# Delta rule loads kept in two fixed sets, half of the first state copies on ScalarE, and two score products moved ahead of values products

## The chip, the cores and the metric

The kernel runs on one core of a Trainium2 chip. The core has five engines that work side by side: TensorE (PE, matrix products into PSUM; its weight loads are shown apart as PEld), VectorE (DVE), ScalarE (ACT), GpSimd (POOL) and SyncE (SP, which here only issues DMA transfers). The metric is the device time of one execution in microseconds (us), a median of several runs. All numbers here come from the runs of the kernel before the change and from the trace of one profiled execution of it.

## What is computed

A two-layer backbone over 512 latent tokens and 256 context tokens of width 1024. Layer 0 mixes tokens with a bidirectional gated delta rule, layer 1 with grouped-query attention (8 query heads, 2 key heads, width 128); each is modulated, gated and added to the stream, and the latent stream is normed at the end. The two places that matter here, cut from the reference:

```python
# layer 0: per head and direction, chunks of 64 tokens, state s (128 x 128)
def step(s, xs):
    qk_i, qd_i, kd_i, u_i, w_i, gl_i = xs
    v_new = u_i - jnp.einsum('bhcd,bhde->bhce', w_i, s)
    o = jnp.einsum('bhcd,bhde->bhce', qd_i, s) + jnp.einsum('bhcs,bhse->bhce', qk_i, v_new)
    s = s * gl_i[..., None, None] + jnp.einsum('bhcd,bhce->bhde', kd_i, v_new)
    return s, o

# layer 1: attention of the latent tokens over context and latent tokens
s = jnp.einsum('bqhgd,bkhd->bhgqk', qg, k).astype(F32) * (d ** -0.5)
p = jax.nn.softmax(s, axis=-1).astype(v.dtype)
return jnp.einsum('bhgqk,bkhd->bqhgd', p, v).reshape(b, lq, hq, d)
```

## The kernel before

**The delta rule.** Both directions run at once: a tile of 128 rows holds one chunk of 64 tokens for the forward direction and one for the backward direction. There are six such tiles (two of context, four of latent tokens) and each is visited twice, with the two halves in exchanged roles, so there are 12 steps; `where(s)` gives the tile and the visit of step `s`. The tiles of steps 0 to 11 are 0, 1, 1, 0, 2, 3, 4, 5, 5, 4, 3, 2. Each step has four units of four value heads (`x = 4 * s + p`), 48 in all. A unit goes through three functions in three successive rounds of one loop: `products(x)` multiplies keys (`kq[0]`) and queries (`kq[1]`) with the state `St` on TensorE, forms `r` on VectorE from the values and `o` on ScalarE, and decays the state on GpSimd; `solve(x)` applies the inverted matrix `T` and copies the new values `vn` and their decayed form `vd`; `update(x)` multiplies with `QK` for the output and with `kt` for the new state, `su`. In one round TensorE gets the products of unit x, the solve of x-1 and the update of x-2, in that order. In step 0 the state is zero, so there are no products with keys and queries, and `su` is copied to the state (line 1660) instead of added.

**Its loads.** `load_step(s)`, called with the first unit of a step, loads from DRAM what the step reads: k, q, kt, `T` and `QK` of 512 KB each, and the values in two transfers of 512 KB. Even steps use one set of buffers (tiles of the pool `even`), odd steps another (tags `T`, `v`, `QK`, `kt`, `kq0` of the pool `ch`), and q has two buffers of its own (`kq1`), used in turn. Every step from 1 on loads everything, also where a set held the same tile before. Only step 0 has its tiles loaded earlier (`opening`). The loads are issued by SyncE.

**What sets the order.** The work of TensorE, VectorE, ScalarE and GpSimd around the change is in an order written out by hand (`written0`, and `written` in layer 1): each of these engines runs its instructions in the order in which the code traces them. SyncE's queue is not written out there; a scheduler orders it. `mark[0]` keeps the last load of a step; the first output weights and gates are issued after it (`tc.issue_after(mark[0])` at units 28, 32, 36 and 40).

**The scores of layer 1.** 32 units `u` (8 heads by 4 tiles of 128 queries) run through a loop. `scores(u)` computes 768 scores per query in three passes of products (the float32 operands are split into a high and a low part). Two units share three PSUM banks in the tile `s3`: each has a bank for itself (`own`, 512 columns) and half of the bank between them (`shared`, 256 columns). Then come `maxima(u)` on VectorE, `powers(u)` (the exponentials, line 2275) on ScalarE, and two units later the transposes `turn`. `values(u2, kts)` multiplies shares with values, half of a pair of units per round of the loop. Up to u = 23 each round also has a projection for TensorE, from u = 26 on a block of the output product; u = 24 and 25 have neither.

Of the kernel before, what the change touches and what calls it, by code (L numbers as in the profile page):

```python
# [8 lines left out]
F32 = mybir.dt.float32  # L9
# [8 lines left out]
P = 128  # L18
# [5 lines left out]
QH, VH = 8, 16  # L24
# [62 lines left out]
def backbone(tc, a, out):  # L87
    nc = tc.nc
    V, S, G, T = nc.vector, nc.scalar, nc.gpsimd, nc.tensor
    dma = nc.sync.dma_start  # L90
# [16 lines left out]
    k_d = dtile([NT, P, QH, P], "k_d")  # L107
    q_d = dtile([NT, P, QH, P], "q_d")
    kt_d = dtile([NT, P, QH, P], "kt_d")
# [4 lines left out]
    t_d = dtile([NT, P, 2, VH, 64], "t_d")  # L114
    qk_d = dtile([NT, P, 2, VH, 64], "qk_d")
# [887 lines left out]

    def matrices_loaded(t, visit, Tt, QK, kt):
        dma(Tt, t_d[t, :, visit])
        dma(QK, qk_d[t, :, visit])
        return dma(kt, kt_d[t]).ins

    def values_loaded(t, v, h0=0, h1=VH):
        p, n, base = pair_info(t)  # L1010
        for hf, c in ((0, p), (1, n - 1 - p)):
            c += base // 64
            dma(v[hf * 64:hf * 64 + 64, h0:h1], v_d[c // 2, c % 2 * 64:c % 2 * 64 + 64, h0:h1])

    def values_tile(s):
        return room["even"].tile([P, 2, 32, 32], F32, tag="C", name=f"cv_{s}").rearrange("p a b c -> p (a b c)").rearrange("p (h d) -> p h d", d=P)

    def even_tile(s, nm):
        return room["even"].tile([P, VH, 64], F32, tag="df", name=f"c{nm}_{s}", bufs=4)

    def by_key_heads(x):
        return x.rearrange("p h c -> p (h c)").rearrange("p (h d) -> p h d", d=P)

    opening = {}
# [117 lines left out]
    last = {}  # L1142
    T0 = 134
# [33 lines left out]
    ck = Piece("DVE", 0.4, 0.0, biases_kept, after=[pv], holds=[("tr", pv)], lands=0.1, slack=0.1)  # L1177
# [17 lines left out]
    for q in range(4):  # L1195
# [7 lines left out]
        for k in (2 * q, 2 * q + 1):  # L1203
            y_ = None
            for i in range(2):
                f = at + 2.5 * (k % 2) + 0.6 * i
# [18 lines left out]
    for k in range(KT):  # L1225
        for h in steps:
            wh, wl = halves_of[h]
            for i in range(2):
                first = not k
# [20 lines left out]
    for h in range(QH):  # L1250
# [4 lines left out]
        else:  # L1255
            wh, wl = k_weights(h, t0)
            g, owners = [], []
            for i in range(2):
                n = 1 if h == 1 else 4
# [28 lines left out]
    c = []  # L1288
# [29 lines left out]
    for n, (i, nb) in enumerate(((0, 4), (0, 5), (1, 0), (1, 2), (1, 1), (1, 3), (1, 4), (1, 5))):  # L1318
# [3 lines left out]
        first, through = nb >= 4 or nb < 2, []  # L1322
# [93 lines left out]
    for pair in range(3):  # L1416
        first = None
# [5 lines left out]
    for t in range(NT):  # L1423
        due = T0 + (185, 80, 315, 190, 30, 335)[t]
        U = [Piece("DVE", 2.15, due, j_turn, t, d, after=[solved[t // 2]] + (joined if t < 5 else []), takes=["U" if t < 5 else "U5"] if d == 0 else (), lands=0.1) for d in range(2)]
        u = U[0].takes[0]
# [96 lines left out]
    if True:  # L1523
        ch.tile([P, 4, P], F32, tag="r0", name="r_0", bufs=1)
        St = [ch.tile([P, 2, 2, P], F32, tag=f"S{hh}", name=f"S{hh}", bufs=1) for hh in range(QH)]
        for tag, shape, n in (("vn", [P, 4, P], 2), ("vd", [P, 4, P], 2), ("T", [P, VH, 64], 1), ("v", [P, VH, P], 1), ("QK", [P, VH, 64], 1),
                              ("kt", [P, QH, P], 1), ("kq0", [P, QH, P], 1), ("kq1", [P, QH, P], 2), ("o", [P, 4, P], 2), ("r1", [P, 4, P], 1)):
            for i in range(n):
                ch.tile(shape, F32, tag=tag, name=f"{tag}_first{i}", bufs=n)

        def where(s):
            n, sl, base = (4, s, 0) if s < 4 else (8, s - 4, 2)
            visit = 0 if sl < n // 2 else 1
            return base + (sl if visit == 0 else n - 1 - sl), visit

        loads = {}
        mark = [None]

        def load_step(s):
            nm = f"_{s}"  # L1540
            t, visit = where(s)
            if s == 0:
                (Tt, QK, kt), v = opening["m"], opening["v"]
                loads[s] = (None, kt, v, Tt, QK)
                return
            if s % 2:
                Tt = ch.tile([P, VH, 64], F32, tag="T", name="cT" + nm, bufs=1)
                v = ch.tile([P, VH, P], F32, tag="v", name="cv" + nm, bufs=1)
                QK = ch.tile([P, VH, 64], F32, tag="QK", name="cQK" + nm, bufs=1)
                kt = ch.tile([P, QH, P], F32, tag="kt", name="ckt" + nm, bufs=1)  # L1550
            k0 = ch.tile([P, QH, P], F32, tag="kq0", name="ck" + nm, bufs=1) if s % 2 else by_key_heads(even_tile(s, "k"))
            if not s % 2:
                Tt, QK = even_tile(s, "T"), even_tile(s, "QK")
                kt, v = by_key_heads(even_tile(s, "kt")), values_tile(s)
            kq = [k0, ch.tile([P, QH, P], F32, tag="kq1", name="cq" + nm)]
            for w, src in enumerate((k_d, q_d)):
                dma(kq[w], src[t])
            values_loaded(t, v)
            mark[0] = matrices_loaded(t, visit, Tt, QK, kt)
            loads[s] = (kq, kt, v, Tt, QK)  # L1560

        live = {}
        prq = [pcx.tile([P, 2, 4, P], F32, tag=tag, name=f"{tag}_all", bufs=1) for tag in ("pr", "pq")]
# [63 lines left out]
        def update(x):  # L1629

            s, p = divmod(x, 4)
            t, visit = where(s)
            kq, kt, v, Tt, QK = loads[s]
            vn, vd = live.pop(x)
            po = prq[x % 2][:, :, 2:4]
            for i in range(2):
                for j in range(2):
                    for hf in range(2):
                        r0, i0 = hf * 64, (hf ^ j) * 64
                        T.matmul(po[r0:r0 + 64, j, i], QK[i0:i0 + 64, 4 * p + 2 * j + i, :], vn[i0:i0 + 64, 2 * j + i], start=True, stop=True)  # L1640
            if s < 11:
                su = pux.tile([P, 2, 2, 2, P], F32, tag="su", name=f"su{x}", bufs=1)
                for j in range(2):
                    hh = 2 * p + j
                    for c0 in (0, 64):
                        for d in range(2):
                            r0 = (visit ^ d ^ j) * 64
                            T.matmul(su[c0:c0 + 64, d ^ j, j], kt[r0:r0 + 64, hh, c0:c0 + 64], vd[r0:r0 + 64, 2 * j:2 * j + 2], start=True, stop=True)  # L1648
            oh = O[t][:, 4 * p:4 * p + 4]
            ov = oh.rearrange("p (j i) d -> p j i d", j=2)  # L1650
            if s == 0:
                S.copy(ov, po)
            else:
                V.tensor_tensor(ov, po, ov, ALU.add)
            if s < 11:
                for j in range(2):
                    hh = 2 * p + j
                    sj = raw(su[:, 0, 0] if j == 0 else su[:, 1, 1], 0, [[512 - 1024 * j, 2], [P, 2], [1, P]])
                    if s == 0:
                        V.tensor_copy(St[hh], sj)  # L1660
                    else:
                        V.tensor_tensor(St[hh], sj, St[hh], ALU.add)  # L1662

# [586 lines left out]
        z_tanh(hq)  # L2250
        z_rest(hq)

    def scores(u):
        hq, t = divmod(u, 4)
        g, b = hq // 4, u % 2
        own, shared = (slice(0, 512), slice(512, 768)) if b == 0 else (slice(256, 768), slice(0, 256))
        for c in (own, shared):
            for n_, (i, j) in enumerate(PASS):
                q = qTs[hq // 2][i][:, hq % 2, t * P:(t + 1) * P]
                T.matmul(s3[:, b, c], q, kT[j][:, g, c], start=n_ == 0, stop=n_ == 2)  # L2260
# [119 lines left out]
    for u in range(32 + 4):  # L2380
# [32 lines left out]
        for half in range(2):  # L2413
            if piece and piece[0] is q_products:
                q_products(*piece[1:], range(half * 4, half * 4 + 4))
            elif piece:
                k0 = 4 * (u % 2) + 2 * half
                z_products(piece[1], range(k0, k0 + 2))
            elif half == 0 and 26 <= u < 33:
                out_block(u - 26, 0, pg)  # L2420
            elif half == 0 and u >= 33:
                s_all = raw(s3, 0, [[1, 3 * 512]])
                acc1 = [s_all[:, nh * 512:(nh + 1) * 512] for nh in range(2)]
                for k in ((0, 1, 2), (3, 4, 5), ())[u - 33]:
                    out_block(k, 1, acc1)
                if u == 35:
                    out_block(7, 0, pg)
            if half == 1 and o is not None:
                q_turned(*last[1:], o)
            if u == 32 and half == 0:  # L2430
                aq_c.__exit__(None, None, None)
                f2_c = tc.tile_pool(name="fo", bufs=2, side="right", reuse_waits="tile")
                f2 = f2_c.__enter__()
                fg = f2.tile([P, D], F32, tag="fg", name="fg", bufs=1)
                gate1 = f2.tile([P, 1, D], F32, tag="gate1", name="gate1", bufs=1)
                ss = f2.tile([P, 4, 3], F32, tag="ss", name="ss", bufs=1)
                dma(gate1, gate_d[1])
                for t in range(3):
                    load_hs(t)
                dma(fg, a["final_norm_g"].unsqueeze(0).partition_broadcast(P).squeeze(1))  # L2440
                G.tensor_scalar(fg, fg, -(2.0 ** 0.5), None, ALU.mult)
            if half == 1 and u >= 4:
                u2, h_ = divmod(u - 4, 2)
                values(u2, range(3 * h_, 3 * h_ + 3))
# [158 lines left out]
```

## Time and profile before

| | us |
|---|---|
| runs shown | 1145.9, 1141.11, 1144.64 |
| median of these | 1144.64 |
| the profiled execution's own time | 1139.69 |
| its span, first to last instruction | 1137.5 |
| the delta rule's stretch in it, about | 535 to 712 |
| the scores' units 24 and 25 in it, about | 1054 to 1062 |

The span of the profiled execution is a little shorter than its time, since the time also has what lies around the instructions. The page of the profile begins with the busy time of each engine; below it stand views of the trace. In a timeline each row is: start in us, duration or stretch in us, engine, line of the code, operation, output <- inputs, shapes (partitions x elements), how many were merged, and in brackets the idle time of the engine just before the row with what ended it. "issue" as a releaser means that the engine waited for nothing that the profile shows. SPq marks DMA transfers as SyncE issues them. The granted clock is the share of full speed at which TensorE was allowed to run (1.00 is full).

### The profile page before, as it was taken

The numbers are of one execution on the slowest core, as the hardware profiler recorded it, in microseconds if no ns is written. First come the engines' busy times: TensorE is split into PE (matmuls) and PEld (weight loads), VectorE is DVE, ScalarE is ACT, GpSimd is POOL, SyncE is SP. The second block draws the span as 40 slices with busy tenths as digits, with TensorE's granted clock in tenths as the row PEclk, the third lists the DMA queues.
The fourth block names the chain that finished last, engine by engine and source line by source line (L and its number), as shares of the span: only waits on it lengthen the run. The fifth ranks groups of instructions, "written<-read, shape, count | busy, mean of one in ns | idle before, by whom it ended". The sixth has DMA issues, their size and how long they took to land. (4 is left out here: it accounts for less than half of the span.)

```text
span 1137.5 us, 27228 instructions
## 1 busy us (share of the span) xinstructions
PE 1106.4 (97%) x10511; PEld 903.7 (79%) x10511; DVE 787.5 (69%) x1628; ACT 746.9 (66%) x1990; POOL 603.1 (53%) x525
## 2 busy tenths in 40 slices
PE   5999999999999999999999999999999999999997
PEld 2677788888888888888666666788877889989886
DVE  4785666688889988774678788445555477667647
ACT  4453554477787888756689888875776356666731
POOL 0564111329999999960675598656744353130820
PEclk9999999999999999999999999999999999999999
DMA  9489753765738887665998994676854112101323
GB/s 366 180 305 324 253 159 118 228 174 171 219 129 245 280 233 222 182 229 164 280 279 249 276 257 116 207 213 183 247 148 139 37 58 73 38 19 57 111 75 93
DMA packets 117106, 208.69 MB, mean 183 GB/s; under 512 B 12113, under 2 KB 76786, under 8 KB 111730
## 3 DMA queue, kind: packets, MB, share of 16 engines
q1 hardware_dynamic: 97202, 195.71, 55.8%
q10 hardware_dynamic: 19776, 11.25, 3.3%
q8 instruction: 83, 1.36, 0.5%
q14 instruction: 45, 0.37, 0.1%
HBM read 166.16 MB, written 40.67 MB: 182 GB/s over the span
## 5 line engine op out<-in xcount | busy, mean ns | idle before, releaser
L1768 PE MATMUL po<-woh,y 128*128 128x512 f32 x384 | 129.3, 401 | 0.0
L1706 POOL TENSOR_TENSOR wol<-wo,woh 128x1024 fp32r<-128x1024 f32 x32 | 77.3, 2416 | 54.3 <-ACT woh L1699 51.1
L810 POOL TENSOR_TENSOR X<-X,tmp 128x62 f32<-128x62 f32 (+15 forms) x93 | 99.5, 1070 | 7.3
L1594 POOL TENSOR_TENSOR S<-S,glb 128x512 f32<-128x512 f32 x80 | 81.8, 1044 | 36.4 <-PE ks L1585 36.1
L809 POOL TENSOR_TENSOR tmp<-L,X 128x62 f32<-128x62 f32 (+15 forms) x93 | 91.0, 979 | 6.7
L929 PE MATMUL g_z<-uh,wh_z 128*128 128x512 f32 (+1 forms) x256 | 88.0, 344 | 0.0
L929 PE MATMUL g_v<-uh,wh_v 128*128 128x512 f32 (+1 forms) x256 | 87.9, 344 | 0.0
L944 DVE SCALAR_TENSOR_TENSOR acc_v<-g_v,cwv,acc_v 128x510 f32<-128x510 f32 (+3 forms) x128 | 77.7, 614 | 14.7 <-ACT acc_v L936 11.3
L929 PE MATMUL g_z<-ul,wh_z 128*128 128x512 f32 (+1 forms) x256 | 86.2, 337 | 0.5 <-issue 0.5
L929 PE MATMUL g_v<-ul,wh_v 128*128 128x512 f32 (+1 forms) x256 | 86.1, 336 | 0.0
L929 PE MATMUL g_v<-uh,wl_v 128*128 128x512 f32 (+1 forms) x256 | 86.1, 336 | 0.0
L929 PE MATMUL g_z<-uh,wl_z 128*128 128x512 f32 (+1 forms) x256 | 86.1, 336 | 0.0
L1768 PEld LDWEIGHTS po<-woh,y 128*128 128x128 f32 x384 | 72.3, 188 | 15.5 <-issue 0.3
L1768 PE MATMUL po<-wol,y 128*128 128x512 f32 x192 | 75.5, 393 | 0.0
L1734 DVE SCALAR_TENSOR_TENSOR pt<-pt,og,z 128x128 f32<-128x128 f32 x96 | 34.4, 358 | 33.3 <-PE pt L1725 31.0
L555 POOL TENSOR_TENSOR kt<-kt,kss 128x768 f32<-128x768 f32 x8 | 11.6, 1472 | 85.6 <-DVE kss L183 57.0
L1585 PE MATMUL ks<-S,ck 128*64 128x256 f32 x352 | 55.5, 392 | 0.9 <-ACT o L1591 0.9
L1662 DVE TENSOR_TENSOR S<-su,S 128x512 f32<-128x512 f32 x80 | 51.5, 686 | 5.1 <-PE su L1648 3.4
L1588 DVE SCALAR_TENSOR_TENSOR r<-ks,negV,cv 128x128 f32<-128x128 f32 x176 | 52.4, 344 | 3.6 <-DMA cv<-v_d 1.9
L1585 PE MATMUL ks<-S,cq 128*64 128x256 f32 x352 | 53.7, 379 | 0.0
L929 PEld LDWEIGHTS g_z<-ul,wh_z 128*128 128x128 f32 x256 | 48.6, 190 | 5.4 <-issue 0.7
L929 PEld LDWEIGHTS g_z<-uh,wh_z 128*128 128x128 f32 x256 | 48.5, 190 | 5.2
(469 smaller groups left out, 3341.5 us busy)
## 6 DMA issues: line engine op xcount, KB each, us to landing
aw<-in_ada_late SPq DMA_DIRECT2D x16, 1024.0 KB, 7.5
wo<-in_dn_w_out SPq DMA_DIRECT2D x32, 512.0 KB, 3.9
cv<-v_d SPq DMA_DIRECT2D x22, 512.0 KB, 9.6
aw<-in_ada_first SPq DMA_DIRECT2D x8, 1024.0 KB, 11.4
w_z<-in_dn_w_in SPq DMA_DIRECT2D x16, 512.0 KB, 6.2
w_v<-in_dn_w_in SPq DMA_DIRECT2D x16, 512.0 KB, 4.8
v_d<-vt ACTq DMA_DIRECT2D x16, 384.0 KB, 4.2
cT<-t_d SPq DMA_DIRECT2D x12, 512.0 KB, 9.1
```

The lines of the kernel that those rows point to most:

```text
L555: G.tensor_tensor(kt, kt, bcast(r[:, h % 2 * NT:(h % 2 + 1) * NT], 2, P), ALU.mult)
L809: G.tensor_tensor(tv, bcast(L[:, :, j + 1:, j], 3, j + 1), bcast(X[:, :, j, 0:j + 1], 2, n), ALU.mult)
L810: G.tensor_tensor(X[:, :, j + 1:, 0:j + 1], X[:, :, j + 1:, 0:j + 1], tv, ALU.subtract)
L929: T.matmul(ps[:, :m], w[:, k], u[:, k, c0:c0 + m], start=k == 0 and n_ == 0, stop=k == KT - 1 and n_ == 2)
L944: V.scalar_tensor_tensor(acc[:, c0 + lo:c0 + hi], ps[:, lo + j - 2:hi + j - 2], cwv[:, j, ct:ct + 1], acc[:, c0 + lo:c0 + hi], ALU.mult, A ...
L1585: T.matmul(ks[r0:r0 + 64, w], kq[w][:, hh, r0:r0 + 64], St[hh][:, d], start=True, stop=True)
L1588: V.scalar_tensor_tensor(r[:, 2 * j + i], ks[:, 0, i], negV[:, visit, t, h:h + 1], v[:, h], ALU.mult, ALU.add)
L1594: G.tensor_tensor(St[hh], St[hh], bcast(g_, 3, P), ALU.mult)
L1662: V.tensor_tensor(St[hh], sj, St[hh], ALU.add)
L1706: G.tensor_tensor(wl, raws.pop(n), halves[n][0], ALU.subtract)
L1734: V.scalar_tensor_tensor(pj, pj, og, raw(z, off, [[st_, 2], [1, 64]]), ALU.mult, ALU.mult)
L1768: T.matmul(acc[nh], y[i][:, j, :], ww[k][:, nh * 512:(nh + 1) * 512], start=h == 0 and x == 0, stop=h == VH - 1 and x == 2)
```

## The change

Three edits.

The delta rule's k, q, values and kt now live in two fixed sets, A and B, named for each step by the string `"ABBABABAABAB"`. Steps 2, 8 and 9 use the set that an earlier step has loaded for the same tile, and load only `T` and `QK`; step 3 loads k and q but keeps the values and kt of step 0. `T` and `QK` still alternate between two buffers. For step 1 the transfer of q is issued behind the values, `T` and `QK`; for the other steps the order is k, q, values, `T`, `QK`, kt. `mark[0]` is now the last transfer that the step has.

In step 0 the second of the two state halves of a unit is copied by ScalarE (`S.copy`), the first still by VectorE.

At u = 24 and 25 the `own` products of the next unit's scores are traced at the start of the half round, ahead of the values products; the next round then traces only the `shared` ones.

```diff
@@ -1523,8 +1523,14 @@
-        for tag, shape, n in (("vn", [P, 4, P], 2), ("vd", [P, 4, P], 2), ("T", [P, VH, 64], 1), ("v", [P, VH, P], 1), ("QK", [P, VH, 64], 1),
-                              ("kt", [P, QH, P], 1), ("kq0", [P, QH, P], 1), ("kq1", [P, QH, P], 2), ("o", [P, 4, P], 2), ("r1", [P, 4, P], 1)):
+        work = [(("vn", [P, 4, P], 2), ("vd", [P, 4, P], 2)), (("o", [P, 4, P], 2), ("r1", [P, 4, P], 1))]
+        odd = {}
+        for tag, shape, n in work[0]:
+            for i in range(n):
+                ch.tile(shape, F32, tag=tag, name=f"{tag}_first{i}", bufs=n)
+        for nm, shape in (("T", [P, VH, 64]), ("v", [P, VH, P]), ("QK", [P, VH, 64]), ("kt", [P, QH, P]), ("k", [P, QH, P]), ("qB", [P, QH, P]), ("qA", [P, QH, P])):
+            odd[nm] = ch.tile(shape, F32, tag=nm, name="c" + nm, bufs=1)
+        for tag, shape, n in work[1]:
             for i in range(n):
                 ch.tile(shape, F32, tag=tag, name=f"{tag}_first{i}", bufs=n)
...
+        (T0, QK0, kt0), v0 = opening["m"], opening["v"]
+        homes = {"A": (by_key_heads(even_tile(0, "k")), odd["qA"], v0, kt0), "B": (odd["k"], odd["qB"], odd["v"], odd["kt"])}
+
         def load_step(s):
-            nm = f"_{s}"
             t, visit = where(s)
+            k, q, v, kt = homes["ABBABABAABAB"[s]]
+            Tt, QK = (odd["T"], odd["QK"]) if s % 2 else (T0, QK0)
+            loads[s] = ((k, q), kt, v, Tt, QK)
             if s == 0:
-                (Tt, QK, kt), v = opening["m"], opening["v"]
-                loads[s] = (None, kt, v, Tt, QK)
                 return
-            if s % 2:
-                Tt = ch.tile([P, VH, 64], F32, tag="T", name="cT" + nm, bufs=1)
...
-            for w, src in enumerate((k_d, q_d)):
-                dma(kq[w], src[t])
-            values_loaded(t, v)
-            mark[0] = matrices_loaded(t, visit, Tt, QK, kt)
-            loads[s] = (kq, kt, v, Tt, QK)
+            fresh = s not in (2, 8, 9)
+            if fresh:
+                dma(k, k_d[t])
+                if s > 1:
+                    dma(q, q_d[t])
+                if s != 3:
+                    values_loaded(t, v)
+            dma(Tt, t_d[t, :, visit])
+            last = dma(QK, qk_d[t, :, visit])
+            if s == 1:
+                dma(q, q_d[t])
+            if fresh and s != 3:
+                last = dma(kt, kt_d[t])
+            mark[0] = last.ins
@@ -1657,7 +1663,7 @@
                     if s == 0:
-                        V.tensor_copy(St[hh], sj)
+                        (S.copy if j else V.tensor_copy)(St[hh], sj)
@@ -2250,11 +2256,13 @@
+    begun = set()
+
-    def scores(u):
+    def scores(u, first=False):
...
-        for c in (own, shared):
+        for c in (own,) if first else (shared,) if u in begun else (own, shared):
@@ -2439,6 +2447,9 @@
+            if half == 0 and u in (24, 25):
+                scores(u + 1, first=True)
+                begun.add(u + 1)
             if half == 1 and u >= 4:
                 u2, h_ = divmod(u - 4, 2)
                 values(u2, range(3 * h_, 3 * h_ + 3))
```

More of the change, by code (lines that the diff above doesn't have):

```diff
@@ L1537, in backbone @@
         mark = [None]
+        (T0, QK0, kt0), v0 = opening["m"], opening["v"]
+        homes = {"A": (by_key_heads(even_tile(0, "k")), odd["qA"], v0, kt0), "B": (odd["k"], odd["qB"], odd["v"], odd["kt"])}
         def load_step(s):
-            nm = f"_{s}"
             t, visit = where(s)
+            k, q, v, kt = homes["ABBABABAABAB"[s]]
+            Tt, QK = (odd["T"], odd["QK"]) if s % 2 else (T0, QK0)
+            loads[s] = ((k, q), kt, v, Tt, QK)
             if s == 0:
-                (Tt, QK, kt), v = opening["m"], opening["v"]
-                loads[s] = (None, kt, v, Tt, QK)
                 return
-            if s % 2:
-                Tt = ch.tile([P, VH, 64], F32, tag="T", name="cT" + nm, bufs=1)
[L1548 to L1555, printed above, removed]
-            for w, src in enumerate((k_d, q_d)):
-                dma(kq[w], src[t])
-            values_loaded(t, v)
-            mark[0] = matrices_loaded(t, visit, Tt, QK, kt)
-            loads[s] = (kq, kt, v, Tt, QK)
+            fresh = s not in (2, 8, 9)
[12 more added lines that the diff above has]
+            mark[0] = last.ins
         live = {}
```

## The prediction

> **What bounds the kernel now.** First the head of the page, which says which engine fills the span, and the stretch of the delta rule (535 to 712 us) in the view of windows. The columns of a window are its length, the busy time of PE, PEld, DVE, ACT and POOL with instruction counts, the granted clock, the DMA share and GB/s.
>
> ```profile
> span 1137.5 us, 27228 instructions
> PE 1106.4 (97%) x10511; PEld 903.7 (79%) x10511; DVE 787.5 (69%) x1628; ACT 746.9 (66%) x1990; POOL 603.1 (53%) x525
> ...
> 557.00:572.00 15.00, 14.09 (x236) 8.91 (x232) 11.58 (x28) 10.67 (x34) 11.07 (x11) 1.00 1.02 284
> 588.00:603.00 15.00, 15.00 (x260) 9.78 (x256) 12.24 (x28) 14.27 (x53) 9.37 (x10) 1.00 0.87 273
> ```
>
> TensorE (PE) bounds it, and it does so inside the delta rule too: 15.00 of 15.00 us busy, while the DMA engines are nearly full (0.87) but in time. So a byte that is not loaded is worth something only where PE waited for it. I look for those places in the timeline of PE. One unit (four value heads of a step) begins with the products of keys and state:
>
> ```profile
> 612.71 0.65 PE L1585 MATMUL ks<-S,ck 128*64 128x256 f32 x4
> 616.48 0.65 PE L1585 MATMUL ks<-S,ck 128*64 128x256 f32 x4
> ...
> 557.30 0.65 PE L1585 MATMUL ks<-S,ck 128*64 128x256 f32 x4
> 560.67 1.13 DVE L1588 SCALAR_TENSOR_TENSOR r<-ks,negV,cv 128x128 f32<-128x128 f32 x4 [1.85 <-DMA cv<-v_d]
> 562.06 0.65 PE L1585 MATMUL ks<-S,ck 128*64 128x256 f32 x4 [0.91 <-ACT o L1591]
> ...
> 569.61 0.65 PE L1585 MATMUL ks<-S,ck 128*64 128x256 f32 x4
> 573.73 0.32 PE L1640 MATMUL pq_all<-vn,cQK 64*64 64x128 f32 x2 [1.16 <-issue]
> 574.96 0.65 PE L1585 MATMUL ks<-S,ck 128*64 128x256 f32 x4
> ...
> 646.68 0.65 PE L1585 MATMUL ks<-S,ck 128*64 128x256 f32 x4
> 651.02 0.65 PE L1585 MATMUL ks<-S,ck 128*64 128x256 f32 x4
> ```
>
> An undisturbed unit takes 616.48 - 612.71 = 3.77 us. Three units are longer. The one from 557.30 takes 4.76: VectorE waited for step 2's values, so 0.99 us too much. The one from 569.61 takes 5.35, 1.58 too much, with PE waiting for nothing that the profile shows, while the DMA engines were full (1.02 in the window above). The one from 646.68 takes 4.34, 0.57 too much. Every other start that I followed from 542 to 708 us keeps the 3.77.
>
> **Reuse of the loads.** With 512 KB in every load of one tensor (values: two of them), steps 2, 8 and 9 each lose k, q, kt and the values (2.5 MB) and step 3 loses kt and the values (1.5 MB): 9 MB in all. The sets are freed when the two buffers are freed now, since a set's next load comes two steps after its last use, so no later load has a shorter window. The first two output weights are tied to the last load of steps 7 and 8; for step 8 that is now QK instead of kt, so one of them leaves a little earlier, and nobody waits for it. I take the three excesses as gone: 0.99 + 1.58 + 0.57 = 3.1 us. The first is sure, as the load is gone. The other two happen beside a full DMA queue, and after the change steps 2, 3, 8 and 9 load far less; if they were something else, 2.1 us of the 3.1 stay.
>
> **The order of step 1's loads** is the part that I hold for decisive. The diff moves q from behind k to behind the values, T and QK. SyncE's timeline and the landing times (last column, us after the issue; the view asked once for each load) of before:
>
> ```profile
> 530.50 0.83 SPq L1557 DMA_DIRECT2D ck<-k_d  x1
> 531.38 0.42 SPq L1557 DMA_DIRECT2D cq<-q_d  x1
> 531.85 1.10 SPq L1013 DMA_DIRECT2D cv<-v_d  x2
> 533.04 0.53 SPq L1005 DMA_DIRECT2D cT<-t_d  x1
> 533.61 0.45 SPq L1006 DMA_DIRECT2D cQK<-qk_d  x1
> ...
> ck<-k_d SPq DMA_DIRECT2D x1, 512.0 KB, 4.1
> cq<-q_d SPq DMA_DIRECT2D x1, 512.0 KB, 6.6
> cv<-v_d SPq DMA_DIRECT2D x2, 512.0 KB, 8.4
> cT<-t_d SPq DMA_DIRECT2D x1, 512.0 KB, 12.8
> cQK<-qk_d SPq DMA_DIRECT2D x1, 512.0 KB, 14.9
> ...
> 542.20 0.65 PE L1585 MATMUL ks<-S,ck 128*64 128x256 f32 x4
> 542.68 0.60 PE L1585 MATMUL ks<-S,cq 128*64 128x256 f32 x4
> ```
>
> They land in the order of issue: k at 534.6, q at 538.0, the values about 540.3, T at 545.8, QK at 533.61 + 14.9 = 548.5. The queue sends them back to back from 530.5 on, so I expect the new order to leave in the same stretch, with as many bytes ahead of the last, and q, now the sixth, to land where QK lands now: 548.5. PE needs it at 542.68, and the products with q stand between those with k: PE stops there, and with it everything behind in its order (the rest of step 0's solves and updates too). That is 548.5 - 542.7 = 5.9 us of wait with the semaphore, which also swallows what the copy below gains. T and QK, which come earlier instead, were not waited for. Bounds: q in time (0) and a landing 2 us later (7.9).
>
> The Trainium skill speaks against this order of landings: in "DMA: Bandwidth & Descriptors", section "Queues, rings and completion order", completion is not first in, first out per issuing engine. By that rule q could be in time and this term 0; the five landings above, all in the order of issue, disagree with it here.
>
> A wait of this length has a second price, which one place of the trace shows:
>
> ```profile
> 24.34 2.08 PE L308 MATMUL rr<-dg,on 128*128 128x512 f32 x2 [3.76 <-DVE dg L303]
> ...
> 22.00:24.00 2.00, 0.00 (x0) 0.00 (x0) 2.00 (x1) 1.50 (x4) 1.74 (x1) 0.90 0.99 410
> 24.00:28.00 4.00, 3.66 (x10) 2.24 (x10) 2.36 (x5) 0.69 (x2) 0.00 (x0) 0.50 1.02 422
> 28.00:32.00 4.00, 4.00 (x22) 1.43 (x21) 3.69 (x15) 1.65 (x4) 0.00 (x0) 0.69 1.02 424
> ```
>
> After 3.76 us without work PE's granted clock is 0.50 for the whole window 24 to 28, and a mean of 0.69 means 0.50 for 2.5 of the next 4 us: about 6.1 us at half speed after the restart, worth up to 3.1 us. My wait is longer than that one, so I expect the same. Bounds 0 and 3.1; I take 2.1, nearer the upper end since this row is the only one, and less than it because the first unit after a wait also waits for VectorE and ScalarE. The rule in the Trainium skill's "TensorE: Matmul & The Clock Gate", section "Part 1: The HAM clock gate", that one busy window of about 3.4 us brings the clock back, would make this term an estimated 1.7 instead.
>
> **Second state halves on ScalarE.** In step 0 PE's second group of state products waits until VectorE has read both halves of the first:
>
> ```profile
> 539.43 1.29 DVE L1660 COPY S<-su 128x512 f32<-128x512 f32 x2
> 539.86 0.59 ACT L1613 COPY vn<-pr_all 128x512 f32<-128x512 f32 x1 [0.80 <-PE pr_all L1611]
> 540.86 1.41 PE L1648 MATMUL su<-vd,ckt 64*64 64x256 f32 x16 [0.64 <-DVE S L1660]
> ```
>
> With one half on each engine the pair is done after about 0.65 instead of 1.29, so PE's wait of 0.64 goes. ScalarE pays four copies of 0.59 (its row for the same shape); the next one on it, vn at 539.86, starts some 0.1 later, and its products come only after the group that waited. So up to -0.64, but only if PE does not wait for q right after: in my sum 0.
>
> **Scores ahead of values.** In the late units of layer 1 PE has no projection to fill with. The view of groups by form for 1050 to 1066, then the timeline and the chain of work:
>
> ```profile
> L2260 PE MATMUL s<-kT,qT 128*128 128x512 f32 x9 | 2.8, 418 | 1.4 <-ACT pr L2275 1.4
> L2260 PE MATMUL s<-kT,qT 128*128 128x256 f32 x12 | 2.1, 281 | 0.0
> ...
> 1058.31 1.31 PE L2260 MATMUL s<-kT,qT 128*128 128x512 f32 x6 [0.79 <-ACT pr L2275]
> 1061.99 1.32 PE L2260 MATMUL s<-kT,qT 128*128 128x512 f32 x6 [0.65 <-ACT pr L2275]
> ...
> 1065.37 1.09 PE po L2309 x9
> 1066.46 1.12 PE s L2260 x6
> ...
> 1106.86 11.20 PE pso L2471 x48
> ```
>
> The 512-column products are the bank that a unit has for itself (`own`), the 256-column ones the bank shared with its neighbour. The wait for ScalarE's reading of the other unit's scores stands before the 512-column form, 1.4 us, and none before the other: `own` already waits for the powers of the unit before, whatever the banks. Placed ahead of the values products it keeps that wait, and those nine products (1.09), which run inside the wait now, are queued behind it. PE then idles 0.79 + 1.09 and does the values afterwards. The unit's scores end about 1.07 later, so the maxima and powers and the next unit's wait move too, and the same happens once more: 2 x 1.07 = +2.1 us. The later end of the values also moves VectorE's gating of them, which stands ahead of the next maxima; some 0.1 of that may show, and I leave it to the range. Behind it PE runs without a gap to the last block (11.20 us of products from 1106.86), so it reaches the end. Bounds: if `own` did not wait, PE would fill 0.7 (its share of 1.12) of each wait: -1.4.
>
> **Sum.** +5.9 (q) + 2.1 (clock) + 2.1 (scores) - 3.1 (excesses) = +7.0 us. The profiled execution took 1139.69 us for its span of 1137.5, the median of the runs shown is 1144.64, 0.4% more; the terms are differences, so I add them to the median: 1151.6 us. Its own range is 1148 to 1155, from the 2.1 that may stay to a lower clock term.
>
> **Rivals.**
> - **q is in time** (not slower): q lands before about 542, because the queue puts it forward or the loads start some 6 us earlier. It decides from a landing at 542.7 on. For it: the order on SyncE's queue is not written out by hand as PE's is, so a load may be sent ahead of its place in the code. Against it: k, q, values, T and QK now go out in the order of the code. Then -0.6 - 3.1 + 2.1 = -1.6: 1143.0. Chance 0.17.
> - **`own` does not wait**, so the split does what it says: +5.9 + 2.1 - 3.1 - 1.4 = +3.5, 1148.1. The row with 1.4 against 0.0 speaks against it. Chance 0.06.
> - **The wait for q is longer** and the clock stays low over more units, with the 2.1 of excess kept: +7.9 + 3.1 + 2.1 - 1.0 = +12.1, 1156.7. Chance 0.05.
> - My forecast: 0.72.
>
> **Chances.** A measurement of this kernel can tell about 0.5% from no change, 5.7 us. Of the forecast's 0.72 I put 0.50 above +5.7 and 0.22 below; the long wait adds 0.05 above. Within 0.5%: 0.22 + 0.06 + 0.12 of the first rival = 0.40, the other 0.05 of which is faster by more. So slower 0.55, same 0.40, faster 0.05. The range 1142 to 1155.5 takes in most of the first rival and leaves out the long wait.
>
> **What would show it.** In the profile of the changed kernel: the products with cq of step 1 wait several us for the DMA cq<-q_d about 542 to 549, and the granted clock falls below 1.0 there; the wait for cv at the second step and the 1.16 us of issue are gone; two waits of PE for ACT pr at L2260's line are near 1.9 us instead of 0.79 and 0.65, ahead of po's products. I am wrong if cq lands before PE reaches it, if the clock stays at 1.0 through a wait over 5 us, or if the split products start before the powers end.

## The result and the profile after

| | before | changed |
|---|---|---|
| median of 8 runs each, us | 1143.28 (1139.08 to 1145.9) | 1148.47 (1147.42 to 1149.74) |
| profiled execution, us | 1139.69 | 1147.42 |
| its span, us | 1137.5 | 1145.5 |
| mean granted clock | 0.995 | 0.991 |

The changed kernel takes 1.0056 times as long, with a 95% interval of 1.0043 to 1.0069: about 6 us more (the two medians alone differ by 5.2). The forecast was 1151.6 us, and its range, 1142 to 1155.5, holds the median.

The head of the page of the changed kernel:

```profile
span 1145.5 us, 27187 instructions
PE 1109.7 (97%) x10511; PEld 906.3 (79%) x10511; DVE 787.6 (69%) x1624; ACT 751.0 (66%) x1994; POOL 603.3 (53%) x525
```

PE has as many instructions as before, so its work has not grown. 8.0 us of span must have come from places where PE stood still or ran slower. The view of waits for PE names the two that are new or have grown (us in total, times, longest; the second was 1.4 in all before the change):

```profile
PE ks L1591 <- DMA cqB<-q_d: 4.2, 1, 4.2
...
PE s L2268 <- ACT pr L2283: 3.4, 2, 1.9
```

The timeline of the changed kernel around step 1, with SyncE's (SPq), VectorE's and ScalarE's rows that bear on it:

```profile
531.52 0.43 SPq L1563 DMA_DIRECT2D cQK<-qk_d  x1
532.00 0.66 SPq L1565 DMA_DIRECT2D cqB<-q_d  x1
...
533.77 0.67 PE L1617 MATMUL pr_all<-cv,cT 64*64 64x128 f32 x16
...
537.82 0.69 DVE L1666 COPY S<-su 128x512 f32<-128x512 f32 x1
538.54 0.59 ACT L1666 COPY S<-su 128x512 f32<-128x512 f32 x1 [1.09 <-DVE S L1666]
539.18 1.08 PE L1654 MATMUL su<-vd,ckt 64*64 64x256 f32 x11 [0.56 <-ACT S L1666]
541.03 0.65 PE L1654 MATMUL su<-vd,ckt 64*64 64x256 f32 x5 [0.77 <-issue]
541.62 0.65 PE L1591 MATMUL ks<-S,ck 128*64 128x256 f32 x4
546.46 1.12 PE L1591 MATMUL ks<-S,cqB 128*64 128x256 f32 x4 [4.18 <-DMA cqB<-q_d]
...
551.97 0.65 PE L1591 MATMUL ks<-S,ck 128*64 128x256 f32 x4
...
710.90 0.65 PE L1591 MATMUL ks<-S,ck 128*64 128x256 f32 x4
```

Its landing times (last column, us after the issue) and its windows (length, the five engines' busy time, granted clock, DMA share, GB/s):

```profile
cQK<-qk_d SPq DMA_DIRECT2D x1, 512.0 KB, 12.7
cqB<-q_d SPq DMA_DIRECT2D x1, 512.0 KB, 14.4
```

```profile
540.00:544.00 4.00, 1.50 (x12) 0.40 (x9) 0.69 (x1) 0.69 (x2) 0.88 (x2) 1.00 1.02 420
544.00:548.00 4.00, 1.54 (x8) 0.98 (x10) 0.38 (x2) 0.00 (x0) 0.33 (x1) 0.53 0.83 237
548.00:552.00 4.00, 4.00 (x57) 2.52 (x54) 0.84 (x3) 2.32 (x6) 2.54 (x4) 0.62 0.44 150
...
550.00:551.00 1.00, 1.00 (x28) 1.00 (x24) 0.00 (x0) 0.96 (x3) 0.42 (x1) 0.50 0.03 12
551.00:552.00 1.00, 1.00 (x22) 0.47 (x16) 0.00 (x0) 0.73 (x2) 0.78 (x2) 0.98 0.49 111
...
1064.00:1068.00 4.00, 2.69 (x14) 2.39 (x12) 2.21 (x4) 1.75 (x4) 4.00 (x3) 0.69 0.64 229
```

QK lands at 531.52 + 12.7 = 544.2 and q at 532.00 + 14.4 = 546.4, in the order of issue. PE starts on q at 546.46. The unit from 541.62 to 551.97 takes 10.35 us where 3.77 is undisturbed. 4.18 of that is the wait, and the other 2.40 go with products at half clock: a group of four products with k or q takes 1.07 to 1.12 instead of 0.60 to 0.65, and the clock's column reads 0.53 and 0.62. In the windows of 1 us it is 0.50 up to 551 and nearly full behind it. The two rows of S show something that the diff doesn't: ScalarE's copy begins at 538.54, just after VectorE's has ended at 537.82 + 0.69 = 538.51. The halves are copied one behind the other, as before.

The late units of layer 1, after the change:

```profile
1059.41 0.81 PE L2296 MATMUL pt<-ident,pr 128*128 128x128 f32 x6
1062.08 0.96 PE L2268 MATMUL s<-kT,qT 128*128 128x512 f32 x3 [1.85 <-ACT pr L2283]
1062.89 1.99 PE L2317 MATMUL po<-pT,vv 128*128 128x256 f32 x9
...
1068.24 0.96 PE L2268 MATMUL s<-kT,qT 128*128 128x512 f32 x3 [1.55 <-ACT pr L2283]
...
1071.02 1.65 PE L2331 MATMUL pg<-wo,yT 128*128 128x512 f32 x6
```

And the marks in the timeline of the kernel before, to measure the same stretches:

```profile
545.97 0.65 PE L1585 MATMUL ks<-S,ck 128*64 128x256 f32 x4
...
707.80 0.65 PE L1585 MATMUL ks<-S,ck 128*64 128x256 f32 x4
...
1055.64 0.82 PE L2288 MATMUL pt<-ident,pr 128*128 128x128 f32 x6
...
1063.73 1.64 PE L2323 MATMUL pg<-wo,yT 128*128 128x512 f32 x6
```

The own scores (the 512-column form) stop PE ahead of the values products, twice, and the nine values products of 1062.89 take 1.99 us instead of 1.30: the clock fell here too (0.69 in the window from 1064), though not before the own scores behind the wait had run at full speed (0.96). With these marks the span is accounted for, PE's start of step 0 being 535.38 before and 533.77 after:

| stretch | before | after | difference |
|---|---|---|---|
| ahead of step 0's first solve | 535.38 | 533.77 | -1.61 |
| step 0's first solve to step 1's first unit | 6.82 | 7.85 | +1.03 |
| step 1's first unit | 3.77 | 10.35 | +6.58 |
| second unit's start to the last unit's start | 161.83 | 158.93 | -2.90 |
| from there to unit 24's transposes | 347.84 | 348.51 | +0.67 |
| unit 24's transposes to the first output block | 8.09 | 11.61 | +3.52 |
| the rest | 73.77 | 74.48 | +0.71 |

They add up to 8.00. The first row and the fifth belong to no part of the change; with the same work ahead of it, step 0 starts between 533.77 and 536.63 in the profiles of all kernels here.

### The profile page after: what moved, and what is told of

Same layout as the page of the kernel before. It is cut to its first block, busy times and chain, and to the rows that moved or that the text cites. A ratio compares the mean times of both kernels' runs of the same rounds, so it can differ in the third digit from the quotient of the medians.

```text
span 1145.5 us, 27187 instructions
## 1 busy us (share of the span) xinstructions
PE 1109.7 (97%) x10511; PEld 906.3 (79%) x10511; DVE 787.6 (69%) x1624; ACT 751.0 (66%) x1994; POOL 603.3 (53%) x525
## 4 chain that ended last, share of the span: by engine, by line
PE 92%; DMA 2%; DVE 2%; ACT 2%; issue 1%; POOL 0%; SPq 0%; ACTq 0%; DVEq 0%; POOLq 0%
PE g_v L929 12%; PE g_z L929 11%; PE po L1774 11%; PE ks L1591 7%; PE g_k L500 6%; PE g_q L929 6%; PE pg L2246 4%; PE pg L2195 4%; PE su L1654 3%; PE po L2317 3%; PE s L2268 3%; PE pa L316 2%; PE kv L2077 2%; PE pt L2296 2%; DMA cqB<-q_d 1%; PE pq_all L1617 1%
## 5 line engine op out<-in xcount | busy, mean ns | idle before, releaser
L929 PEld LDWEIGHTS g_z<-uh,wl_z 128*128 128x128 f32 x256 | 48.5, 189 | 5.3
L929 PEld LDWEIGHTS g_v<-uh,wh_v 128*128 128x128 f32 x256 | 48.5, 190 | 5.1
```

Source lines behind the costliest of these rows:

```text
L929: T.matmul(ps[:, :m], w[:, k], u[:, k, c0:c0 + m], start=k == 0 and n_ == 0, stop=k == KT - 1 and n_ == 2)
```

## The experiments

The theory after the traces: the late q costs 6.6 us, the split of the scores 3.9, the reuse of the loads gives 2.9 back, and ScalarE's copies do nothing. (The 3.9 runs from unit 24's transposes to the end of the first output block, 1072.91 - 1059.41 against 1065.20 - 1055.64; the table's 3.52 stops at that block's start.) Three kernels undo one part or all but one, and a fourth moves q by one place; four more follow. Each ratio is to the kernel before, timed beside it; 0.001 is 1.14 us. The intervals reach 0.0013 to 0.002 to either side, so a difference of two ratios is good to about 2 us.

**q behind k.** Only the place of the load changes.

```
             if fresh:
                 dma(k, k_d[t])
-                if s > 1:
-                    dma(q, q_d[t])
+                dma(q, q_d[t])
...
-            if s == 1:
-                dma(q, q_d[t])
```

> The changed kernel with q of step 1 put back behind k; the rest of the change stays. Theory: the wait for q (4.18 us) and the low clock behind it (first unit 10.35 us against 3.77 undisturbed, so 2.4 us beside the wait) are the order's whole price, so about 6.6 us go: 1148.5 - 6.6 = 1141.9 us, no wait of PE for the q load, clock 1.00 from 540 to 560. Rival: T and QK, now later, are waited for in q's place (T is needed some 5 us after q), so 2 us or less go: 1146.5 us or more.

Measured: 1141.41 us, ratio 0.9995 (0.9979 to 1.0012). Timeline and landing time of this kernel:

```profile
542.69 0.65 PE L1651 MATMUL su<-vd,ckt 64*64 64x256 f32 x5 [1.06 <-issue]
543.75 0.60 PE L1588 MATMUL ks<-S,cqB 128*64 128x256 f32 x4
...
1054.12 0.82 PE L2293 MATMUL pt<-ident,pr 128*128 128x128 f32 x6
1056.79 0.96 PE L2265 MATMUL s<-kT,qT 128*128 128x512 f32 x3 [1.85 <-ACT pr L2280]
...
1061.52 0.97 PE L2265 MATMUL s<-kT,qT 128*128 128x512 f32 x3 [1.71 <-ACT pr L2280]
...
1064.31 1.64 PE L2328 MATMUL pg<-wo,yT 128*128 128x512 f32 x6
```

```profile
cqB<-q_d SPq DMA_DIRECT2D x1, 512.0 KB, 8.8
```

No wait for q, full clock, and no wait for T or QK in its place: the rival falls. From 1.0056 to 0.9995 the order of one load costs 0.0061, 7.0 us. The late rows show a second thing. Both waits of the split are there, but here the clock held (the stretch is 1064.31 - 1054.12 = 10.19 us, 2.10 more than before, against 3.52 more in the changed kernel's profile). So 2.1 us is the price of the split without the clock, and what the clock adds differs between the profiles.

**No split of the scores.** The three lines that call `scores(u + 1, first=True)` are taken out; q stays late.

> The changed kernel with the scores of units 25 and 26 behind the values products again; the late q stays. Theory A (own waits for the powers of the unit before, and the price is the 3.9 us by which the stretch from the transposes of unit 24's predecessor to the first output block grew in the trace, of which 1.2 are a lower clock after the longer wait): 1148.5 - 3.9 = 1144.6 us, PE's waits for the powers back at 0.8 and 0.65, clock 1.00 in that stretch. Theory B (the prediction's size, 2.1 us): 1146.4 us. Rival (the split saves time, and the stretch grew for another reason): 1149 us or more.

Measured: 1144.6 us, ratio 1.0029 (1.0013 to 1.0044). Against 1.0056 the split costs 0.0027, 3.1 us, between theory A's 3.9 and theory B's 2.1. The intervals are too wide to choose; a clock that falls in some executions and not in others would give such a mean. The waits are back:

```profile
PE ks L1591 <- DMA cqB<-q_d: 5.2, 1, 5.2
...
PE s L2268 <- ACT pr L2283: 1.4, 2, 0.8
```

The wait for q, in the same code, was 4.18 in one profile and 5.2 here, partly because PE came to it with less of a stall ahead (0.34 us of issue against 0.77). Beside this wait the first unit, from 541.96 to 552.86, is 10.90 - 3.77 - 5.18 = 1.95 us too long: the clock.

**The sets alone.** q behind k, no split, VectorE copies both halves.

> The changed kernel with q behind k, no split of the scores, and both state halves copied by VectorE: only the reuse of the loads is left of the change. Theory: 1148.5 - 6.6 - 3.9 = 1138.0 us, which is the kernel before less its three long units (2.9 us) and some scatter, so 1138 to 1141 us. Rival (the long units come from something else than the loads): one or two of them are back, and the time is that of the kernel before, 1143 us.

Measured: 1138.09 us, ratio 0.9967 (0.9953 to 0.9982): faster than the kernel before by 3.8 us (3.0 by the two medians), as the theory says, and the rival falls. The reuse is the part that pays. From the second unit's start to the last unit's the trace has 708.77 - 549.57 = 159.20 us against 161.83. It still has a stall that the kernel before hardly shows:

```profile
541.18 1.08 PE L1651 MATMUL su<-vd,ckt 64*64 64x256 f32 x10 [0.64 <-DVE S L1663]
543.88 1.12 PE L1651 MATMUL su<-vd,ckt 64*64 64x256 f32 x6 [1.62 <-issue]
```

The clock fell in this stall as well: the six products behind it take 1.12 us, where the same six took 0.66 in the run below with the own scores in a tile of their own. This profile was of the slowest of the kernel's runs, 1140.81 us.

**q ahead of QK.** The changed kernel with q one place earlier, to see whether wait and clock follow the landing.

```
             dma(Tt, t_d[t, :, visit])
+            if s == 1:
+                dma(q, q_d[t])
             last = dma(QK, qk_d[t, :, visit])
-            if s == 1:
-                dma(q, q_d[t])
```

> The changed kernel with q of step 1 one place earlier, ahead of QK instead of behind it. Theory: loads land one after the other, so q lands where QK landed in the changed kernel (12.7 us behind its issue, about 544.2), and PE waits 1.5 to 2 us instead of 4.18; if the clock falls only after a longer wait, the low clock goes too: 1148.5 - 2.3 - 2.4 = 1143.8 us; if a wait of that length already lowers the clock, 1146.2 us. Rival (landing order does not follow the issue): the wait stays near 4 us and the time near 1148.5 us.

Measured: 1144.42 us, ratio 1.0024 (1.0008 to 1.0041).

```profile
541.76 0.65 PE L1591 MATMUL ks<-S,ck 128*64 128x256 f32 x4
545.22 1.12 PE L1591 MATMUL ks<-S,cqB 128*64 128x256 f32 x4 [2.81 <-DMA cqB<-q_d]
...
548.66 0.61 PE L1646 MATMUL pr_all<-vn,cQK 64*64 64x128 f32 x16
...
550.06 0.65 PE L1591 MATMUL ks<-S,ck 128*64 128x256 f32 x4
```

```profile
cqB<-q_d SPq DMA_DIRECT2D x1, 512.0 KB, 12.9
```

q lands 1.2 us earlier than in the changed kernel and PE's wait falls from 4.18 to 2.81; the landing follows the place on the queue. The wait is longer than expected for two reasons of about 0.4 us each. Counted from step 0's first solve (534.34 here, 533.77 in the changed kernel), PE reaches step 1 earlier (7.42 against 7.85), since it stalled less on the way (0.37 instead of 0.77), and q lands later than QK did in this place (10.85 against 10.45). The clock still falls: 550.06 - 541.76 - 3.77 - 2.81 = 1.72 us beside the wait. The median came out nearer the case without a low clock (1143.8) than the other (1146.2), but the profile shows the low clock, and the interval is too wide to hold the median against it.

**ScalarE's copies on top of the sets alone.** One line: `(S.copy if j else V.tensor_copy)` instead of `V.tensor_copy`.

> The kernel of the run with the sets alone, and ScalarE's copies of the second state halves back. Prediction's size with q in time: PE's wait of 0.64 us ahead of the second state products goes, 0.6 us less than with the sets alone (1138.1 less 0.6). Theory after the traces: ScalarE's copy starts only when VectorE's copy of the same state products has ended (538.54 against 537.82 in the changed kernel), so the pair takes 1.3 us as before and the wait stays at 0.56 to 0.57: the same time as with the sets alone, within 1 us.

Measured: 1139.64 us, ratio 0.9966 (0.9947 to 0.9986), against 0.9967 without. The intervals could not show the 0.6 us of the prediction; the trace does: PE's wait is 0.56 instead of 0.64, so it has not gone.

```profile
542.03 1.08 PE L1651 MATMUL su<-vd,ckt 64*64 64x256 f32 x11 [0.56 <-ACT S L1663]
```

**Own scores in a tile of their own.** The changed kernel's own scores waited for the powers of the unit before although their bank is another one. Is it the bank or the tile? Here, on the sets alone, unit 25 has its own scores ahead of the values in `pg[0]`, another tile; it is therefore read in two parts.

```
+                to = pg[0] if u == 25 and c == own else s3[:, b, c]
-                T.matmul(s3[:, b, c], q, kT[j][:, g, c], ...
+                T.matmul(to, q, kT[j][:, g, c], ...
...
+            if half == 0 and u == 24:
+                scores(25, first=True)
+                begun.add(25)
```

> The kernel with the sets alone, and of the late units unit 25 alone has its own scores ahead of the values; these own scores go to a tile of PSUM that no other unit's scores use, and unit 25 reads its scores in two parts. Theory: in the changed kernel the own scores waited for the powers of the unit before because both were in one tile, not because the engine needs it; so here the own scores of unit 25 start right behind the transposes of unit 22 or 23 with no wait, the values follow, and only the shared scores wait: the 0.79 us of wait at unit 25 shrinks below 0.3, and the clock stays at 1.00. The parted reads cost ScalarE and VectorE some 0.5 us, which may lengthen unit 26's wait (0.65) by as much: time within 1 us of the sets alone (1138.1). Rival: the own scores wait 1.8 us again ahead of the values, and the time is 1 to 2 us above the sets alone.

Measured: 1141.74 us, ratio 0.9989 (0.9971 to 1.0007).

```profile
1053.45 0.95 PE L2266 MATMUL pg<-kT,qT 128*128 128x512 f32 x3
...
1054.02 7.03 POOL L2483 TENSOR_TENSOR wo<-wf,wo 128x1024 fp32r<-128x1024 f32 x3
1054.22 2.19 DVE L2281 TENSOR_TENSOR nm<-mx,sq 128x1 f32<-128x1 f32 x1
...
1057.58 0.63 PE L2266 MATMUL s<-kT,qT 128*128 128x256 f32 x3 [2.12 <-ACT pr L2299]
...
1061.81 1.44 PE L2266 MATMUL s<-kT,qT 128*128 128x512 f32 x6 [1.88 <-ACT pr L2295]
```

The own scores start with no wait right behind the transposes, so the mechanism is as the theory says. But the time isn't: the shared scores wait 2.12 us and unit 26's scores 1.88, and behind the second wait the clock falls (the mean is 0.71 from 1064 to 1068), which the theory had at 1.00. The experiment brought its own disturbance, since I had put the maxima into SBUF. VectorE's `nm`, on 128 x 1 elements, lasts 2.19 us and ends at 1056.41. GpSimd's three operations from 1054.02 take 7.03 / 3 = 2.34 each, so its first ends at 1056.36. The Trainium skill's "SBUF — State Buffer", section "Who interferes with whom", fits that: VectorE and GpSimd share a pair of SBUF ports as an exclusive lock, and an operation of VectorE with two operands in SBUF has to wait for a GpSimd operation that reads SBUF.

**The same with the small results in PSUM.** `mx` and the second sum lie in unused columns of `s3`, as the maxima lie in PSUM in the kernel before.

> As the run with unit 25's own scores in a tile of their own, but the small results of its reductions lie in PSUM again, where the kernel before has them. In the run before this one VectorE's nm took 2.19 and 2.11 us with its operands in SBUF, while GpSimd worked, against 0.16 us in the kernel with the sets alone. Theory: with nm at 0.16 again the own scores run with no wait, the wait of unit 25's shared scores is 0.79 less about 0.64 of own scores ahead of it, so below 0.3 us, the parted reads lengthen unit 26's wait from 0.65 to some 1.2 us, the clock stays at 1.00: within 1 us of the sets alone, 0.9967 of the kernel before, and 2 to 3 us less than the run before this one. Rival: the parting itself was what cost, waits stay near 2 us and the ratio near 0.999.

Measured: 1137.7 us, ratio 0.9964 (0.9948 to 0.9981): within the intervals the same as the sets alone (0.9967) and the sets with ScalarE's copies (0.9966), and faster than both kernels.

```profile
1054.63 0.94 PE L2266 MATMUL pg<-kT,qT 128*128 128x512 f32 x3
1055.40 0.16 DVE L2281 TENSOR_TENSOR nm<-s,sq 128x1 f32<-128x1 f32 x1
...
1056.73 0.64 PE L2266 MATMUL s<-kT,qT 128*128 128x256 f32 x3
...
1060.49 1.33 PE L2266 MATMUL s<-kT,qT 128*128 128x512 f32 x6 [1.42 <-DVE sm L2297]
```

`nm` is at 0.16 again, unit 25's wait is gone, and unit 26's grows from 0.65 to 1.42 through the parted reads. From unit 24's transposes to the first output block it is 8.17 us, against 8.08 with the sets alone: the idea of the split works once the own scores have a tile of their own, and its gain is paid back by the next unit. So it brings nothing beyond the sets.

**Without T and QK of step 1.** What is the stall without a named cause in step 0's second state products?

```
+            if s == 1:
+                G.memset(Tt, 0.0)
+                G.memset(QK, 0.0)
+            else:
                 dma(Tt, t_d[t, :, visit])
                 last = dma(QK, qk_d[t, :, visit])
```

> The kernel with the sets alone, without step 1's loads of T and QK: GpSimd fills both with zeros instead, so this part of the computation is left out and 1 MB less is loaded at 530 to 548 us. It asks what the stall without a named cause in step 0's second state products is (issue, 1.62 us with the sets alone, 0.3 to 1.1 in the other runs). Theory: PE's next instructions are fetched over the same DMA engines as the loads, and come late while these are full; with fewer loads the stall shrinks below 0.3 us and the clock stays at 1.00: some 2 us less in the stretch from step 0's first solve to step 1's first unit. Rival: it belongs to this place in the program and stays between 0.3 and 1.6 us.

Measured: 1138.12 us, ratio 0.9956 (0.9935 to 0.9977).

```profile
540.76 1.09 PE L1655 MATMUL su<-vd,ckt 64*64 64x256 f32 x16 [0.64 <-DVE S L1667]
```

```profile
540.00:544.00 4.00, 3.36 (x51) 2.04 (x48) 2.64 (x7) 1.00 (x3) 3.58 (x5) 1.00 1.01 324
```

The stall is gone and the clock holds, but the DMA engines are as full as ever (1.01): SyncE sent the next loads (kt, and q of step 2) at once in the place of the two. The run did not take away what it meant to, so it doesn't tell the theory from its rival. Nor would its missing stall alone: the kernel of the last section, with all loads, has a stall of only 0.16 there.

## Why the prediction was right, point by point

| term | predicted | in the trace | by the runs |
|---|---|---|---|
| wait for q | +5.9 | +4.18 | with the clock 7.0 |
| clock behind it | +2.1 | +2.40 | |
| split of the scores | +2.1 | +3.52 | 3.1 |
| three long units | -3.1 | -2.90 | sets alone -3.8 |
| ScalarE's copies | 0 | -0.08 | 0 |
| stall in step 0 | none | +1.11 | |
| sum | +7.0 | +8.2 | 0.0056, 6.4 |

The stall and the copies together are the +1.03 of the table above; the stretches that the change doesn't touch take 0.2 off again (-1.61 + 0.67 + 0.71), which leaves the 8.0 of the spans. The sum came out better than its terms: q's wait was put 1.7 too high, the scores 1.4 too low and the stall was not foreseen, and that these partly cancel is luck. Of the 3.1 us by which 1151.6 lies above the measured 1148.47, 1.4 are the base: the three runs shown had a median of 1144.64, all eight have 1143.28.

- **The order of step 1's loads** was decisive, as forecast, and the rival that q is in time fell: all loads that I followed landed in the order of issue. The step mis-sized is "to land where QK lands now: 548.5". q landed at 546.4. Of these 2.1 us, 1.5 are that the whole stretch ran earlier in this execution (k is issued at 529.02 instead of 530.50). PE came to q only 0.4 earlier, since a stall of 0.77 that I hadn't foreseen stood ahead of it. Part of the wait was thus only called otherwise, and in the run with less of that stall the wait was 5.2. The rule in the Trainium skill's "DMA: Bandwidth & Descriptors", section "Queues, rings and completion order", that completion isn't first in, first out, changed the order of none of these 512 KB loads.
- **The clock** fell as the one row of the trace had shown, and 2.1 was near the three traces with a wait for q: 2.40, 1.95 (5.2 us of wait) and 1.72 (2.81). What the prediction had not seen is how long the clock stays low. Worked out from windows of 0.2 us it was at half for 6.83 us in the changed kernel (544.20 to 551.03), for 6.83 without the split and for 3.42 with q ahead of QK, and it fell while PE was still waiting. From PE's restart on that leaves 4.57, 3.67 and 3.19 us at half clock, an estimated price of 2.3, 1.8 and 1.6, close to the three measured. The rule of one busy window of about 3.4 us in the Trainium skill's "TensorE: Matmul & The Clock Gate", section "Part 1: The HAM clock gate", agrees with these lengths, one or two windows, if the window is not counted from PE's restart; the Trainium skill calls it free-running there. In the changed kernel the restart at 546.46 lies within the first of two such windows, and the second was the first that was busy throughout.
- **The scores.** The step held: own waits for the powers of the unit before, the values stand behind it, and without a fall of the clock the stretch is 2.10 us longer, as forecast. What failed is that I gave only the long wait for q a clock term: a wait of 1.85 us was followed by a fall as well, 1.4 us more in the changed kernel's profile. The reason that I gave, "whatever the banks", is now shown: the unit before does not read that bank in either case, and with a tile of its own the wait is gone. So the program guards `s3` as one tile.
- **The copies.** "With one half on each engine the pair is done after about 0.65" is wrong, though its 0 in the sum was right. Each half spans both banks of `su`, and the program lets VectorE finish first. The Trainium skill's "PSUM — Partial Sum Buffer", section "PSUM bank collisions raise a hardware error", says why it must: two engines may not access one bank on the same partitions at once, reads included. The trace agrees, with 0.03 us between the end of one copy and the start of the other; no run here lets them overlap, and none tells whether the shared banks or the shared tile made the program order them.
- **The excesses** went as priced, 2.90 of 3.1; a unit of 3.99 us at 676.55 in the changed kernel is new. That every other start keeps the 3.77 was not quite so: the unit from 703.87 took 3.93 before, and takes 3.93 after, from 706.97. What I missed is that a stall without a named cause came up at another place: 0.77 us in step 0 of the changed kernel, and 0.16 to 1.62 us in the other profiles of changed kernels with the full set of loads. Three kernels that are the same up to that point (the sets alone, and the two with a tile of its own) had 1.62, 0.74 and 0.16, so its size is not the code's alone. Its cause stays open.

## What to carry to other kernels

When loads of one step are reordered, price the place of each load in the queue against the first product that needs it: one 512 KB load moved behind four others of its step cost 7.0 us here, and leaving out 9 MB of loads gave 3.8. A split that starts work early on an engine that runs in order pays only if the work moved ahead really has nothing to wait for; look for who still reads the same tile, not only the same bank. A wait on TensorE costs more than its length where the clock falls behind it, and around waits of 1.5 to 2.1 us it fell in some of the profiles and not in others.

## What the runs showed of the hardware that I had not expected

- There is no single length of wait from which the clock falls. It stayed full behind 1.55 us (second wait of the split), 1.71 and 1.85 us (the run with q behind k) and 2.12 us (the run with a tile of its own and nm in SBUF). It fell during a stall of 1.62 us (sets alone), and about 1 us behind waits of 1.85 us (changed kernel, q ahead of QK) and 1.88 us (tile of its own, nm in SBUF).
- Once fallen, the clock stayed at half for 3.4 us or for twice that, 6.8, and for no other length, in all ten traces up to 1130 us (worked out from the mean clock of windows of 0.2 us). What a fall costs thus depends on how much of this time PE has work: least when it falls early in a wait.
- An operation of VectorE on 128 x 1 elements took 2.19 and 2.11 us with all operands in SBUF while GpSimd worked, and 0.16 and 0.22 us with only one left in SBUF and the rest in PSUM.
